# The low part of the weight last in the down units between pairs, and the sixth down weight's split moved behind the first chunk's addition

## The chip, the core and the metric

The kernel runs on one core of a Trainium2 chip. Its metric is the device time of one execution in microseconds (us). A core has five engines that matter here: PE (TensorE, matrix products into PSUM), DVE (VectorE), ACT (ScalarE), POOL (GpSimd) and SP (SyncE, which issues most loads). Each engine takes its instructions strictly in the order in which they stand in its queue, and they wait for each other by semaphores. The order in each queue is decided when the program is built.

## What is computed

One inference step of a decoder with two layers, on 512 new prompt tokens and 8 sample tokens (520 columns), width 1024:

```python
for i in range(DEPTH):                       # 2 layers: attention, then gated linear attention
    mp, ... = swa_prompt(...) / gla_mix(...)
    x = layer_norm(ALPHA * x + mix, ...)
    h = x @ w_up                             # (1024 -> 2 * 2816): gate a and value u
    c = conv_b + sum(conv_w[j] * ap[:, j:j + T] for j in range(3))
    y = (gelu(c) * u) @ w_down               # 2816 -> 1024
    x = layer_norm(ALPHA * x + y, ...)
```

All of it is in float32. What matters here is the second half of each layer, the gated feed-forward part, and the layer norm behind it.

## The kernel before

**Products.** Activations lie transposed, with the features on the partitions: 8 blocks of 128 features. Tokens are in two groups, a (256 columns) and b (264). A product of float32 precision is made of three matrix products in the fast format fp32r: a weight is split into a high part h (`wh`) and a low part l (`wl`), an activation into `hh` and `hl` (or `xh`, `xl`), and a block takes h·hh + h·hl + l·hh. A unit of work is one weight tile of 128x1024 with its two parts. Units are loaded ahead; six pairs of `wh`/`wl` buffers turn round (WSLOTS = 6), and two buffers for the raw weight.

**Two ways to a low part.** ACT copies the raw weight into `wh` (rounding it), and then either DVE subtracts (L200, L314: `wl` = raw - `wh`), or ACT writes -`wh` into `wl` (L205) and POOL issues a DMA that adds the weight from memory onto it (L206, `low_by_dma`). The weights of the down units between pairs take the second way.

**The feed-forward part.** Its 2816 features are 22 blocks j. The first four blocks are made by plain gate and value units; from j = 4 on, a gate and a value are made together by `ffn_pair` (seven half products, L308 to L310). The down product is done in five parts of 4, 4, 4, 2 and 8 blocks. The weights of the first four parts are spread over 14 units, one behind each pair from j = 4 to j = 17 (`ffn_down2`, L919 to L921). Such a unit of the first three parts makes two output chunks m and m + 1 for each group: 2 chunks x 4 blocks x 3 products = 24 matmuls into the two halves of one PSUM tile `widep`, group a and then group b, and DVE adds both halves to x at once (L924 or L926). The low product stands third for each block:

```python
for s in range(2):
    for k in range(nk):
        nc.tensor.matmul(o, h[:, ks], rh, ...)    # L919
        nc.tensor.matmul(o, h[:, ks], rl, ...)    # L920
        self.final = nc.tensor.matmul(o, l[:, ks], rh, ...)   # L921
```

**The last down products.** Behind pair 21 stand the eight units of the last part (`ffn_down`, one output chunk m each). The first four chunks of group a (the heads, L938) are begun together, and end with the products that need block 21. Then comes `ln_chunk`: DVE adds chunk m to x (L335); for m = 0 PE sums the columns of the sum (L341, tile `sc`), ACT reads that out (L343, `sb`), and DVE and POOL subtract it from x (L350). Then follow chunk 4, the chunks of group b and so on in turn. The products with the fifth and the sixth weight are L236 and L238 (high), with the low part's in one run at the end (L243).

**Releases.** Loads are not timed; a load is issued where a unit releases its buffer (`release`, `load_next`), and the split's instructions are put into the queues of ACT and DVE there. In the last pair (j = 21) releases are held back (`self.held`) and given out at its end: two behind the last addition of its products, and three (`kinds[1:]`: two units, one half buffer) behind its last instructions on ACT and DVE, by `issue_after`, which only sets the order in which a planner places instructions. So the splits of the fifth and the sixth down weight stand on DVE behind the last split of the activations.

Of the kernel before, what the change touches and what calls it, by code (L numbers as in the profile page):

```python
# [15 lines left out]
ALU = mybir.AluOpType  # L16
# [69 lines left out]
def in_turn(rows):  # L86

    return rows.rearrange("p t j -> p j t")
# [10 lines left out]
class Net:  # L99
# [226 lines left out]
    def ln_chunk(self, g, m, ps, scaled, last=False):  # L326


        nc, n, x = self.nc, g.n, g.x
        t = lambda name: self.ln.tile([P, g.n], F32, name=f"{name}_{g.name}")  # L330
        c = lambda name, b=1: self.ln.tile([P, NT - 256], F32, name=name, bufs=b)[:, :n]
        if m:
            yield 0
        if scaled:
            nc.vector.scalar_tensor_tensor(x[:, m], x[:, m], self.back[:, m:m + 1], ps, op0=ALU.add, op1=ALU.add)  # L335
        else:
            nc.vector.scalar_tensor_tensor(x[:, m], x[:, m], ALPHA, ps, op0=ALU.mult, op1=ALU.add)
        if m == 0:
            yield 1
            mp = self.mtile("sc")[:, :n]  # L340
            nc.tensor.matmul(mp, self.ones_a, x[:, 0], start=True, stop=True)  # L341
            sb = c("sb")
            nc.scalar.activation(sb, mp, AF.Copy, scale=float(KD))  # L343
            sa = sb
            if not scaled:
                sa = c("sa")
                nc.scalar.activation(sa, mp, AF.Copy, scale=KD / ALPHA)
            for i in range(KD):
                eng = nc.gpsimd if i else nc.vector
                eng.tensor_tensor(x[:, i], x[:, i], sa if i else sb, op=ALU.subtract)  # L350
            g.s2 = t("s2")
            nc.scalar.activation(g.s2, x[:, 0], AF.Square)
            return
        q = c("sq", 2)
        sq = nc.scalar.activation(q, x[:, m], AF.Square)
        if m == 6 and g.i == 0:
            with self.tc.issue_after(sq.ins):
                nc.scalar.preload_act_table_set("natural_log_exp_and_others")
        if last and m == KD - 1:

            g.q = q
            return
        if m == 1:
            g.s1 = t("s1")

        p1, p2 = (KD - 1, KD - 1) if g.i and not last else (0, S2P)
        (nc.gpsimd if m < p1 else nc.vector).tensor_tensor(g.s1, x[:, 0] if m == 1 else g.s1, x[:, m], op=ALU.add)
        (nc.gpsimd if m < p2 else nc.vector).tensor_tensor(g.s2, g.s2, q, op=ALU.add)
# [452 lines left out]
    def ffn_pair(self, u, layer, j, q):  # L821


        nc, W = self.nc, self.w[u]
        a, b = self.groups
        if j == PAIRED:
            self.plain = False
            self.row_sum1()
            self.close(self.cp_cm)
            self.cp, self.cp_cm = self.open(f"merged{layer}")  # L830
            self.m = [self.cp.tile([P, 2, 2 + NT], F32, name=f"merged{i}") for i in range(2)]
            self.c = [self.cp.tile([P, 2, NT - 256], F32, name=f"conv{i}") for i in range(2)]
            for t in self.m:
                nc.gpsimd.memset(t[:, 0, 0:2], 0.0)
            self.close_psum()
            self.open_wide()
        if j == NF - 1:
            self.held = []
        half = KD // 2
        part = lambda g, ks: (g.xh[:, ks], g.xl[:, ks])  # L840
        lo, hi = slice(0, half), slice(half, KD)
        t1, (t2, t3, t4) = part(b, lo), zip(self.th, self.tl)
        n, m = a.n, b.n
        add = lambda o, x, y: nc.vector.tensor_tensor(o, x, y, op=ALU.add)
        M, C = self.m[j % 2], self.c[j % 2]
        both = lambda x: x.unsqueeze(1).broadcast_to([P, 2, x.shape[-1]])
        g, h = M[:, 0], M[:, 1, 2:]
        p1 = self.one.tile([P, 512], F32, name="onep")
        with self.tc.issue_after(self.final) if j < PAIRED + ORDERED else ExitStack():
            self.half_product(p1, W["a11"], part(a, lo), n)  # L850
        v = self.ln.tile([P, NT - 256], F32, name="nv")[:, :n]
        nc.scalar.copy(v, p1[:, :n])
        p = self.wide()
        self.half_product(p[:, 0], W["a12"], part(a, hi), n)
        self.release()
        self.half_product(p[:, 1], W["s2"], t2, m)
        add(M[:, :, 2:2 + n], p[:, :, :n], both(v))
        nc.scalar.copy(h[:, n:m], p[:, 1, n:m])
        p = self.wide()
        products = [(p[:, 0], W["s1"], t1, m), (p[:, 1], W["a22"], t4, n)]  # L860
        for x in reversed(products) if j == PAIRED else products:
            self.half_product(*x)
        self.release()
        add(C[:, :, :n], p[:, :, :n], both(h[:, :n]))
        add(C[:, 0, n:], p[:, 0, n:m], h[:, n:m])
        p = self.wide()
        self.half_product(p[:, 0], W["s4"], part(b, hi), m)
        if j != NF - 2:
            self.release()
        self.half_product(p[:, 1], W["s3"], t3, m)  # L870
        self.release("half")
        add(M[:, :, 2 + n:], p[:, :, :m], both(C[:, 0]))
        summed = add(h[:, :n], p[:, 1, :n], C[:, 1, :n])
        w, cb = self.taps(layer, j)
        c = C.rearrange("p a b -> p (a b)")[:, :NT]
        nc.scalar.activation(c[:, :SEQ], g[:, 2:2 + SEQ], AF.Identity, scale=w(2), bias=cb)
        nc.vector.scalar_tensor_tensor(c[:, :SEQ], g[:, 1:1 + SEQ], w(1), c[:, :SEQ], op0=ALU.mult, op1=ALU.add)
        nc.vector.scalar_tensor_tensor(c[:, :SEQ], g[:, 0:SEQ], w(0), c[:, :SEQ], op0=ALU.mult, op1=ALU.add)
        nc.vector.scalar_tensor_tensor(c[:, SEQ:], g[:, 2 + SEQ:], w(2), self.base[:, j], op0=ALU.mult, op1=ALU.add)
        self.pcopy(self.nconv_p[:, j], g[:, SEQ:2 + SEQ])  # L880
        self.pcopy(self.nconv_s[:, j, :, 1], g[:, 2 + SEQ:])
        nc.scalar.activation(c, c, AF.Gelu)
        nc.vector.scalar_tensor_tensor(h, c, -1.0, h, op0=ALU.mult, op1=ALU.mult)
        self.split(a.hh[:, q], a.hl[:, q], parted(h[:, :n]))
        self.split(b.hh[:, q], b.hl[:, q], parted(h[:, n:]))
        if j == NF - 1:
            kinds, self.held = self.held, None
            done = [next(x for x in reversed(nc.cur_bb.bb.instructions) if x.engine == engine)
                    for engine in (mybir.EngineType.Activation, mybir.EngineType.DVE)]
            with self.tc.issue_after(summed.ins):  # L890
                self.release()
                self.release(kinds[0])
            with self.tc.issue_after(done[0]), self.tc.issue_after(done[1]):
                for kind in kinds[1:]:
                    self.release(kind)
            nc.scalar.dma_start(out=self.O["conv_p"][layer], in_=self.nconv_p)
            nc.scalar.dma_start(out=self.O["conv_s"][layer], in_=self.nconv_s)
            for cm in (self.cp_cm, self.pp_cm, self.fp_cm):
                self.close(cm)
            self.close_psum()  # L900
            self.open_acc()

    def ffn_down2(self, u, layer, part, i):


        nc = self.nc
        h, l = self.w[u]
        j0, j1 = FF_PARTS[part]
        nk = j1 - j0
        ms = KD // nk  # L910
        for g, m in ((g, ms * i + m) for g in self.groups for m in range(0, ms, 2)):
            ps, n = self.wide(), g.n
            for s in range(2):
                o = ps[:, s, :n].rearrange("p (j t) -> p j t", t=2)
                for k in range(nk):
                    t, q = (m % ms + s) * nk + k, self.place(j0 + k)
                    ks = slice(t * P, t * P + P)
                    rh, rl = in_turn(g.hh[:, q]), in_turn(g.hl[:, q])
                    nc.tensor.matmul(o, h[:, ks], rh, start=k == 0, stop=False)  # L919
                    nc.tensor.matmul(o, h[:, ks], rl, start=False, stop=False)  # L920
                    self.final = nc.tensor.matmul(o, l[:, ks], rh, start=False, stop=k == nk - 1).ins  # L921
            x = g.x[:, m:m + 2]
            if part == 0:
                nc.vector.scalar_tensor_tensor(x, x, ALPHA, ps[:, :, :n], op0=ALU.mult, op1=ALU.add)  # L924
            else:
                nc.vector.tensor_tensor(x, x, ps[:, :, :n], op=ALU.add)  # L926
# [566 lines left out]
```

## Time and profile before

| | us |
|---|---|
| median of 3 runs | 1099.82 |
| the three runs | 1105.21, 1098.45, 1099.82 |
| the profiled execution | 1098.55 |
| its span, first to last instruction | 1096.6 |
| PE busy | 1058.9 (97%) |
| DVE busy | 882.0 (80%) |
| ACT busy | 663.1 (60%) |
| POOL busy | 303.1 (28%) |
| mean granted TensorE clock | 0.994 |

The profiled execution took 1.95 us more than its span, for what lies around the first and the last instruction. A matmul here lasts about 0.28 us from its start to its end, but the next one starts about 0.11 us after it, so that PE's busy time says little of its pace: gaps between starts do. In a row of the time line stand start, length, engine, line, operation, tiles and shapes, the count, and in brackets the idle time before it with what ended it.

### The profile page before, as it was taken

What the parts mean: (1) busy time and instruction counts of PE and PEld (TensorE: products, weight loads), DVE (VectorE), ACT (ScalarE), POOL (GpSimd) and SP (SyncE); (2) the same over time, 40 slices, a digit from 0 to 9 for tenths busy, and PEclk for the clock granted to TensorE, in tenths of its full rate; (3) what the DMA queues carried; (4) which work ended last, traced back from release to release, by engine and by line L of the source; (5) the groups of instructions that cost most, each with busy time, mean ns of one, the idle gap of its engine ahead of it and who ended that gap; (6) DMA issues with size and microseconds to landing.
All of it is one profiled execution on the core that took longest, in us unless ns stands there. A gap on an engine that the chain in (4) does not pass through costs nothing.

```text
span 1096.6 us, 23781 instructions
## 1 busy us (share of the span) xinstructions
PE 1058.9 (97%) x9174; PEld 1031.2 (94%) x9174; DVE 882.0 (80%) x1797; ACT 663.1 (60%) x1308; POOL 303.1 (28%) x512
## 2 busy tenths in 40 slices
PE   8999999999999999999899999999999999999996
PEld 8997899999999999999799899899999999999995
DVE  7897668988778878978667678778988788888975
ACT  5677667766655665547545456458776655655643
POOL 4576562221111110274111100362221111110163
PEclk9999999999999999999999999999999999999998
DMA  7554048587777774437224364558588777774412
GB/s 233 147 173 125 21 128 207 135 215 191 180 177 178 176 174 116 124 130 204 66 74 145 115 185 136 164 170 215 134 205 197 180 174 177 175 185 116 116 66 79
DMA packets 65472, 167.44 MB, mean 153 GB/s; under 512 B 8104, under 2 KB 28624, under 8 KB 65360
## 3 DMA queue, kind: packets, MB, share of 16 engines
q1 hardware_dynamic: 50960, 119.47, 33.8%
q0 software_dynamic: 12240, 44.57, 23.1%
q10 hardware_dynamic: 2160, 1.89, 0.5%
q8 instruction: 72, 1.18, 0.4%
q14 instruction: 40, 0.33, 0.1%
HBM read 153.24 MB, written 8.47 MB: 147 GB/s over the span
## 4 chain that ended last, share of the span: by engine, by line
PE 66%; DVE 13%; DMA 10%; ACT 5%; issue 5%; SPq 1%; POOL 0%; DVEq 0%; ACTq 0%; POOLq 0%
PE widep L308 8%; PE widep L310 8%; PE widep L309 8%; PE accp L236 6%; PE accp L238 6%; PE accp L240 6%; PE widep L921 5%; PE widep L920 5%; PE widep L919 5%; DMA vb<-dv 2%; DMA wl<-in_w_up 2%; DVE wl L200 2%; PE onep L310 1%; PE onep L309 1%; PE onep L308 1%
## 5 line engine op out<-in xcount | busy, mean ns | idle before, releaser
L313 ACT ACTIVATE wh<-raw 128x1024 fp32r<-128x1024 f32 x72 | 76.2, 1061 | 98.7 <-PE widep L920 57.3
L194 ACT ACTIVATE wh<-raw 128x1024 fp32r<-128x1024 f32 (+1 forms) x92 | 96.0, 1047 | 52.3 <-PE accp L238 19.4
L309 PE MATMUL widep<-tl,wh 128*128 128x264 f32 (+1 forms) x432 | 119.1, 276 | 0.0
L310 PE MATMUL widep<-th,wl 128*128 128x264 f32 (+1 forms) x432 | 119.1, 276 | 0.0
L308 PE MATMUL widep<-th,wh 128*128 128x264 f32 (+1 forms) x432 | 119.1, 276 | 0.0
L236 PE MATMUL accp<-xh_b,wh 128*128 128x264 f32 x400 | 113.1, 283 | 2.6 <-DVE hprod L817 2.6
L240 PE MATMUL accp<-xh_b,wl 128*128 128x264 f32 x400 | 111.5, 279 | 0.0
L236 PE MATMUL accp<-xs_a,wh 128*128 128x256 f32 x400 | 106.1, 285 | 5.4 <-DVE sg L1202 2.5
L238 PE MATMUL accp<-xl_b,wh 128*128 128x264 f32 x384 | 107.5, 280 | 0.0
L206 POOL DMA_DIRECT2D wl<-in_w_down x28 | 24.3, 866 | 293.6 <-ACT wl L205 271.0
L238 PE MATMUL accp<-xs_a,wh 128*128 128x256 f32 x384 | 103.1, 284 | 0.5
L314 DVE TENSOR_TENSOR wl<-raw,wh 128x1024 fp32r<-128x1024 f32 x72 | 87.5, 1218 | 7.5 <-ACT wh L313 7.5
L205 ACT ACTIVATE wl<-wh 128x1024 fp32r<-128x1024 f32 x85 | 89.1, 1051 | 1.0
L200 DVE TENSOR_TENSOR wl<-raw,wh 128x1024 fp32r<-128x1024 f32 (+2 forms) x64 | 79.0, 1244 | 12.3 <-ACT wh L194 11.5
L236 PEld LDWEIGHTS accp<-xs_a,wh 128*128 128x128 f32 x400 | 76.7, 195 | 7.0 <-DVE sg L1202 2.9
L308 PEld LDWEIGHTS widep<-th,wh 128*128 128x128 f32 x432 | 82.1, 190 | 0.0
L309 PEld LDWEIGHTS widep<-tl,wh 128*128 128x128 f32 x432 | 82.1, 190 | 0.0
L310 PEld LDWEIGHTS widep<-th,wl 128*128 128x128 f32 x432 | 82.1, 190 | 0.0
L236 PEld LDWEIGHTS accp<-xh_b,wh 128*128 128x128 f32 x400 | 75.7, 189 | 4.3 <-DVE hprod L817 3.4
L308 PE MATMUL widep<-xh_b,wh 128*128 128x264 f32 x288 | 79.6, 276 | 0.0
L309 PE MATMUL widep<-xl_b,wh 128*128 128x264 f32 x288 | 79.5, 276 | 0.0
L310 PE MATMUL widep<-xh_b,wl 128*128 128x264 f32 x288 | 79.5, 276 | 0.0
(419 smaller groups left out, 4113.1 us busy)
## 6 DMA issues: line engine op xcount, KB each, us to landing
raw<-in_w_up SPq DMA_DIRECT2D x88, 512.0 KB, 4.0
wl<-in_w_up POOLq DMA_DIRECT2D x52, 512.0 KB, 7.1
raw<-in_w_down SPq DMA_DIRECT2D x44, 512.0 KB, 3.9
wl<-in_w_down POOLq DMA_DIRECT2D x28, 512.0 KB, 6.5
raw<-in_w_gla SPq DMA_DIRECT2D x24, 512.0 KB, 3.5
raw<-in_w_mix_o SPq DMA_DIRECT2D x16, 512.0 KB, 4.1
qs<-hl SPq DMA_DIRECT2D x64, 64.0 KB, 2.1
sgla<-in_state_gla SPq DMA_DIRECT2D x16, 256.0 KB, 2.9
```

The costliest lines, as they stand in the source:

```text
L194: nc.scalar.activation(h[:, c], r[:, c], AF.Copy)
L200: nc.vector.tensor_tensor(l[:, c], r[:, c], h[:, c].bitcast(F32), op=ALU.subtract)
L205: self.nc.scalar.activation(l, h.bitcast(F32), AF.Copy, scale=-1.0)
L236: nc.tensor.matmul(o, h[:, ks], xh, start=k == 0, stop=False)
L238: nc.tensor.matmul(o, h[:, ks], xl, start=False, stop=False)
L240: nc.tensor.matmul(o, l[:, ks], xh, start=False, stop=not tail and k == nt - 1)
L308: self.nc.tensor.matmul(o, h[:, ks], rh, start=k == 0, stop=False)
L309: self.nc.tensor.matmul(o, h[:, ks], rl, start=False, stop=False)
L310: self.final = self.nc.tensor.matmul(o, l[:, ks], rh, start=False, stop=k == KD // 2 - 1).ins
L313: self.nc.scalar.activation(hi, src, AF.Copy)
L314: self.nc.vector.tensor_tensor(lo, src, hi.bitcast(F32), op=ALU.subtract)
L919: nc.tensor.matmul(o, h[:, ks], rh, start=k == 0, stop=False)
```

## The change

Two things. In `ffn_down2`, the products of both halves with the high part come first, and those with the low part in one run at the end. And of the three releases that the last pair gave out at its end, only the first (`kinds[1]`, the fifth weight) stays there; the other two are kept and given out in `ln_chunk`, behind the addition of chunk 0 of group a.

```diff
         if scaled:
-            nc.vector.scalar_tensor_tensor(x[:, m], x[:, m], self.back[:, m:m + 1], ps, op0=ALU.add, op1=ALU.add)
+            first = nc.vector.scalar_tensor_tensor(x[:, m], x[:, m], self.back[:, m:m + 1], ps, op0=ALU.add, op1=ALU.add)
+            if m == 0 and g.i == 0:
+                with self.tc.issue_after(first.ins):
+                    for kind in self.kept:
+                        self.release(kind)
...
             with self.tc.issue_after(done[0]), self.tc.issue_after(done[1]):
-                for kind in kinds[1:]:
-                    self.release(kind)
+                self.release(kinds[1])
+            self.kept = kinds[2:]
...
-            for s in range(2):
+            for low, s in ((0, 0), (0, 1), (1, 0), (1, 1)):
...
                     rh, rl = in_turn(g.hh[:, q]), in_turn(g.hl[:, q])
+                    if low:
+                        self.final = nc.tensor.matmul(o, l[:, ks], rh, start=False, stop=k == nk - 1).ins
+                        continue
                     nc.tensor.matmul(o, h[:, ks], rh, start=k == 0, stop=False)
                     nc.tensor.matmul(o, h[:, ks], rl, start=False, stop=False)
-                    self.final = nc.tensor.matmul(o, l[:, ks], rh, start=False, stop=k == nk - 1).ins
```

Three places show what this does to the queues. PE's queue at the first `ffn_down2` unit of layer 0, group a (`widep` is the PSUM tile, `hs_a` holds the activations' two parts), before:

```order
L310 MATMUL widep_3397<-th_2730,wl_3313 128x264
L919 MATMUL widep_3530<-hs_a,wh 128x256
L920 MATMUL widep_3530<-hs_a,wh 128x256
L921 MATMUL widep_3530<-hs_a,wl 128x256
L919 MATMUL widep_3530<-hs_a,wh 128x256
L920 MATMUL widep_3530<-hs_a,wh 128x256
L921 MATMUL widep_3530<-hs_a,wl 128x256
```

The end of the same 24 products in the changed kernel, where L926, L927 and L924 are the former L919, L920 and L921 (eight such couples of L926 and L927 stand ahead of the run of eight):

```order
L926 MATMUL widep_3530<-hs_a,wh 128x256
L927 MATMUL widep_3530<-hs_a,wh 128x256
L926 MATMUL widep_3530<-hs_a,wh 128x256
L927 MATMUL widep_3530<-hs_a,wh 128x256
L924 MATMUL widep_3530<-hs_a,wl 128x256 x8
L926 MATMUL widep_3556<-hh_b,wh 128x264
```

The first use of `wl` moved from the third place to the seventeenth.

DVE's queue behind pair 21 of layer 0, at the fifth and the sixth down weight (`wl_6619`, then `wl_6625`), before:

```order
L314 TENSOR_TENSOR hl_b_93<-merged1_3383,hh_b_92 128x264
L200 TENSOR_TENSOR wl_6619<-raw_6617,wh_6618 128x1024
L200 TENSOR_TENSOR wl_6625<-raw_6623,wh_6624 128x1024
L335 SCALAR_TENSOR_TENSOR x_a_86<-x_a_86,back_85,accp_6642 128x256
L350 TENSOR_TENSOR x_a_86<-x_a_86,sb_6739 128x256
```

The same place in the changed kernel (the sixth weight's low part is now `wl_6730`, and L354 the former L350):

```order
L314 TENSOR_TENSOR hl_b_93<-merged1_3383,hh_b_92 128x264
L200 TENSOR_TENSOR wl_6619<-raw_6617,wh_6618 128x1024
L335 SCALAR_TENSOR_TENSOR x_a_86<-x_a_86,back_85,accp_6636 128x256
L200 TENSOR_TENSOR wl_6730<-raw_6728,wh_6729 128x1024
L354 TENSOR_TENSOR x_a_86<-x_a_86,sb_6739 128x256
```

The addition L335 changed places with the sixth weight's subtraction; the sixth weight's copy on ACT and its load on SP stand where they stood. Layer 1 shows the same two moves. The planner moved one more thing, in each layer: ACT's queue behind pair 16, before:

```order
L876 ACTIVATE conv_3384<-merged_3382,par 128x512
L882 ACTIVATE conv_3384<-conv_3384 128x520
L313 ACTIVATE wh<-raw 128x1024
L852 COPY nv<-onep 128x256
L313 ACTIVATE hs_a<-merged_3382 128x2x128
```

And in the changed kernel (L880, L886 and L856 are the former L876, L882 and L852):

```order
L880 ACTIVATE conv_3384<-merged_3382,par 128x512
L313 ACTIVATE wh<-raw 128x1024
L886 ACTIVATE conv_3384<-conv_3384 128x520
L856 COPY nv<-onep 128x256
L313 ACTIVATE wh<-raw 128x1024
L313 ACTIVATE hs_a<-merged_3382 128x2x128
```

There a weight's copy (L313) went ahead of the GELU, and a second one ahead of the split of block 16's product. DVE's queue follows it with the same weights' subtractions. Beside this, two transposes in the second layer's mixer stand one matmul later on PE; POOL and SP keep their order.

## The prediction

> **What bounds the kernel.** I read the page first, its busy times and the chain that ended last.
>
> ```profile
> PE 1058.9 (97%) x9174; PEld 1031.2 (94%) x9174; DVE 882.0 (80%) x1797; ACT 663.1 (60%) x1308; POOL 303.1 (28%) x512
> PE 66%; DVE 13%; DMA 10%; ACT 5%; issue 5%; SPq 1%; POOL 0%; DVEq 0%; ACTq 0%; POOLq 0%
> ```
>
> PE carries two thirds of the chain. The change takes no matmul away, so it can only shorten stretches in which PE waits. The list of PE's waits says what there is to win. Its columns are who waited for whom, the total in us, how often, and the longest.
>
> ```profile
> PE accp L236 <- DVE sg L1202: 2.5, 1, 2.5
> PE sc L341 <- DVE x_a L335: 2.5, 2, 1.4
> PE accp L236 <- ACT wh L194: 2.3, 3, 1.4
> ...
> PE widep L921 <- DMA wl<-in_w_down: 2.0, 2, 1.1
> ```
>
> Two of these rows name the places that the change touches: the low product L921 waits twice for the low part's DMA, and the column sum L341 waits twice for the addition L335. Twice each, so once per layer. That is 4.5 us in 1096.6, or 0.4%: the waits that the change touches do not hold 1%. The other two rows stand in the mixers, between the feed-forward parts; I need them below.
>
> **The down units: the first unit's wait.** The time line of PE at the first `ffn_down2` unit of each layer:
>
> ```profile
> 223.62 0.27 PE L919 MATMUL widep<-hs_a,wh 128*128 128x256 f32 x1
> 223.73 0.28 PE L920 MATMUL widep<-hs_a,wh 128*128 128x256 f32 x1
> 224.92 0.38 PE L921 MATMUL widep<-hs_a,wl 128*128 128x256 f32 x1 [0.92 <-DMA wl<-in_w_down]
> 225.14 0.28 PE L919 MATMUL widep<-hs_a,wh 128*128 128x256 f32 x1
> ...
> 227.48 0.28 PE L919 MATMUL widep<-hh_b,wh 128*128 128x264 f32 x1
> ...
> 800.08 0.27 PE L919 MATMUL widep<-hs_a,wh 128*128 128x256 f32 x1
> 800.19 0.28 PE L920 MATMUL widep<-hs_a,wh 128*128 128x256 f32 x1
> 801.57 0.38 PE L921 MATMUL widep<-hs_a,wl 128*128 128x256 f32 x1 [1.10 <-DMA wl<-in_w_down]
> 801.78 0.28 PE L919 MATMUL widep<-hs_a,wh 128*128 128x256 f32 x1
> ```
>
> From 225.14 to 227.48 there are 21 matmuls: 2.34 / 21 = 0.111 us from one start to the next. From L920 at 223.73 to the second L919 at 225.14 there are two steps, which should take 0.22 and took 1.41: the wait cost 1.19. In layer 1 it is 801.78 - 800.19 - 0.22 = **1.37**.
>
> In the changed kernel 16 high products stand ahead of the first low one: it comes up at 223.62 + 16 x 0.111 = 225.40 and at 800.08 + 1.78 = 801.86. The low part was there by 224.92 and 801.57, when L921 began. So it is early by 0.48 and 0.29, and both waits go whole. A landing later by d than this costs d minus that margin, at most what the wait cost before. The other units have nothing to give, as the group of L921 over the whole of layer 0's pairs shows: one idle stretch in 112 matmuls of group a.
>
> ```profile
> L921 PE MATMUL widep<-hs_a,wl 128*128 128x256 f32 x112 | 30.9, 276 | 0.9 <-DMA wl<-in_w_down 0.9
> ```
>
> What does the new order cost PE? It goes to and fro between the two halves of `widep` with two more switches per couple of chunks: 12 units x 2 groups + 2 units x 4 couples = 32 couples in a layer, 64 in both, 128 switches. The 21 matmuls above contain one such switch and show no step longer than 0.01 us over the pace; so 0 to 0.01 each, 0 to 1.3 us in all. Eight low products in one run exist already (L243), at (1.06 - 0.28) / 7 = 0.111 each:
>
> ```profile
> 474.88 1.06 PE L243 MATMUL accp<-hs_a,wl 128*128 128x256 f32 x8
> ```
>
> I take 0 for the order. The unit's last reader of `wh` comes 8 low products earlier, and ACT's copy of a later weight, which waits for such readers, may start some 0.9 us earlier:
>
> ```profile
> L313 ACT ACTIVATE wh<-raw 128x1024 fp32r<-128x1024 f32 x72 | 76.2, 1061 | 98.7 <-PE widep L920 57.3
> ```
>
> That ACT waits there 57.3 us in total says that it has time; PE never waits for these copies between 225.14 and 472.56, so nothing is won. DVE adds both halves at once, behind the last low product as before.
>
> **The sixth weight.** DVE and PE behind pair 21, layer 0 and then layer 1:
>
> ```profile
> 469.75 2.36 DVE L200 TENSOR_TENSOR wl<-raw,wh 128x1024 fp32r<-128x1024 f32 x2 [0.50 <-ACT wh L194]
> 472.03 0.47 DVE L335 SCALAR_TENSOR_TENSOR x_a<-x_a,back,accp 128x256 f32<-128x256 f32 x1
> 473.71 0.42 DVE L350 TENSOR_TENSOR x_a<-x_a,sb 128x256 f32<-128x256 f32 x1 [1.21 <-ACT sb L343]
> ...
> 469.87 0.28 PE L938 MATMUL accp<-hs_a,wl 128*128 128x256 f32 x1
> ...
> 470.87 0.28 PE L938 MATMUL accp<-hs_a,wl 128*128 128x256 f32 x1
> 472.56 0.70 PE L341 MATMUL sc<-x_a,ones_a 128*128 128x256 f32 x2 [1.41 <-DVE x_a L335]
> ...
> 1046.07 2.36 DVE L200 TENSOR_TENSOR wl<-raw,wh 128x1024 fp32r<-128x1024 f32 x2 [0.51 <-ACT wh L194]
> 1048.34 0.47 DVE L335 SCALAR_TENSOR_TENSOR x_a<-x_a,back,accp 128x256 f32<-128x256 f32 x1
> ...
> 1047.52 0.28 PE L938 MATMUL accp<-hs_a,wl 128*128 128x256 f32 x1
> 1048.87 0.70 PE L341 MATMUL sc<-x_a,ones_a 128*128 128x256 f32 x2 [1.08 <-DVE x_a L335]
> ```
>
> The first head ended at 469.87 + 0.28 = 470.15, so chunk 0 lay ready for 1.9 us while DVE subtracted two weights. Two subtractions took 472.03 - 469.75 = 2.28 from start to start, one takes 1.14. In the changed kernel one is left ahead: L335 starts at 470.89. PE followed 0.53 behind L335's start (472.56 - 472.03), so L341 starts at 471.42, **1.14** earlier; PE is free for it at 470.87 + 0.11 = 470.98 and still waits 0.44. In layer 1: 2.27 / 2 = **1.14** as well, L341 at 1047.73, free at 1047.63. At most the whole of these waits could go, 1.58 and 1.24.
>
> What is late next? L350 needs `sb`, 1.68 behind L335's start. The sixth subtraction now stands between: 0.4 + 1.14 = 1.54 behind that start DVE is free again, 0.14 before it is needed. Were it later, this would cost the difference, on DVE first. The sixth weight's low part is finished near 470.9 + 1.6 = 472.5; the chain has PE at the run of products that reads it here:
>
> ```profile
> 480.42 0.89 PE accp L243 x8
> ```
>
> At 479.3 in the changed kernel, then: a cover of nearly 7 us. Its copy on ACT and its load stand where they stood, so the load's start does not move against the copy.
>
> **Pair 16.** The GELU goes behind a weight's copy, about 1 us by the 1061 ns above. What hangs on it is block 16 of the last down part, which PE reads some 50 us later (pair 16 is near 400, the heads end at 470.87). Cost nothing; without that cover it would be 1.06 us per layer. The DVE moves there bring two weights forward. The two transposes in the mixer move by one matmul, 0.11 us, in a stretch where PE does other products: nothing.
>
> **The sum.** 1.19 + 1.37 + 1.14 + 1.14 = 4.84 us. Against the profiled execution's own 1098.55 this gives 1093.7; that execution lies 1.27 under the median of the three runs shown, 1099.82, against which it would be 1095.0. I predict **1094.3**, between the two. Behind each saving PE runs on at its pace, and the loads, splits and additions are released by PE's own progress, so that what it wins should move everything behind it.
>
> **Rivals.**
> *Given back in the second mixer.* Layer 0's saving, 1.19 + 1.14 = 2.33, passes through the linear attention, where PE waits 2.5 us for DVE (L1202) and 1.4 for ACT at a weight. If those waits end by loads in flight rather than by PE's progress, they grow by what was won. Then 1098.55 - 2.51 = 1096.0. For it: the waits are there and are long. Against it: the loads are released by PE and the norm ahead. 13%.
>
> *The low part's wait stays in part.* A landing later by over 0.3 to 0.5 us, from another state of the queues, gives back up to 2.56: 1096.3. For it: margins of 0.29 and 0.48 are small beside the 6.5 us that such a transfer takes from issue to landing (the last column, a median):
>
> ```profile
> wl<-in_w_down POOLq DMA_DIRECT2D x28, 512.0 KB, 6.5
> ```
> Against it: in layer 0 nothing ahead of the load has changed. 8%.
>
> *The clock.* Three stretches in the second mixer, by engine's busy time, with the granted clock in PEclk:
>
> ```profile
> 540.30:543.73 3.43, 0.90 (x7) 0.58 (x6) 2.88 (x9) 2.01 (x9) 0.13 (x1) 1.00 0.00 0
> 543.73:547.14 3.41, 3.41 (x19) 3.41 (x18) 2.46 (x5) 0.97 (x4) 3.41 (x8) 0.50 0.50 154
> 547.14:550.50 3.36, 3.36 (x32) 3.36 (x32) 2.36 (x8) 1.57 (x5) 0.58 (x2) 1.00 0.00 0
> ```
>
> After a stretch in which PE was busy for 0.90 of 3.43 us, the clock was half for 3.41 us: 19 matmuls where the next stretch has 32, some 1.7 us lost. If the shift splits the idle time otherwise, this stretch may go: 1093.7 - 1.7 = 1092.0, 12%. Or others come: the wait for ACT above, 1.4 us, and two more of that size would have to fall so. **Slower than before** it becomes from three such stretches more: 1093.7 + 3 x 1.7 = 1098.8, and 0.25 over its own time before; 4%. [...]
>
> *It doesn't do what it says.* The queues show both moves, so the waits can't stay in their old form. 1%.
>
> **How the numbers follow.** The forecast has the remaining 62%, at 1093.7 to 1095.0. The cases of a gain end at 1092.0 and 1096.3; 1.3 us of switches on top gives 1097.6; and single runs of the kernel before lay 1.37 apart in two of three, the third 5.4 higher, so that a median may sit a little above its sum. The range is 1091.0 to 1098.5. A change of 1%, 11 us, is about what a measurement of this kernel can tell from none; it would need more than twice the waits that the change touches, or on the slow side more than anything named here. Faster by over 1%: 0.02; within 1%: 0.95; slower by over 1%: 0.03.
>
> **What would show it.** In the changed profile the waits of the low product for `wl` are gone or under 0.3 us, and no other PE wait stands in the pairs' stretch; L341 waits 0.3 to 0.5 us in layer 0 and about 0.1 in layer 1; both stretches from the first down unit to L341 are shorter by 1.2 + 1.1 and 1.4 + 1.1; the mixers take the time they took, give or take a half-clock stretch. I am wrong if the first low product still waits, if L335 waits for something else than DVE's queue, or if the second mixer has become longer by what the first layer won.

## The result, and the profile after

| | before | after |
|---|---|---|
| median, us (22 runs each) | 1099.61 | **1096.16** |
| lowest and highest run, us | 1095.85, 1105.21 | 1093.50, 1099.52 |
| the profiled execution, us | 1098.55 | 1097.34 |
| its span, us | 1096.6 | 1095.5 |

The ratio is 0.9968, 95% interval 0.9960 to 0.9977: 3.5 us less, between 2.5 and 4.4. The forecast was 1094.3, from a sum of 4.84 us.

The two profiled executions differ by only 1.21 us, so I did not compare ends. I cut the span at two of PE's instructions in each layer: the first matmul of the first down unit, and the column sum of chunk 0 behind pair 21. The view that sums busy time over given stretches then gives, for the kernel before (columns: stretch, its length, busy time of PE, PEld, DVE, ACT, POOL, the granted clock, DMA share, GB/s):

```profile
223.62:472.56 248.94, 246.61 (x2199) 246.23 (x2197) 206.56 (x350) 148.95 (x219) 34.78 (x73) 1.00 0.70 173
472.56:800.08 327.52, 317.26 (x2660) 304.75 (x2661) 255.09 (x574) 193.36 (x427) 93.74 (x138) 0.99 0.51 143
800.08:1048.87 248.79, 246.61 (x2198) 246.23 (x2196) 206.76 (x350) 149.01 (x219) 33.38 (x65) 1.00 0.69 170
```

and for the changed kernel:

```profile
225.86:472.54 246.68, 246.52 (x2198) 246.22 (x2196) 205.76 (x350) 150.87 (x219) 36.15 (x73) 1.00 0.70 173
472.54:800.72 328.18, 316.71 (x2661) 303.38 (x2662) 255.94 (x575) 193.44 (x427) 94.05 (x138) 1.00 0.51 143
800.72:1047.69 246.97, 246.54 (x2198) 246.22 (x2196) 205.67 (x350) 150.94 (x219) 34.61 (x65) 1.00 0.69 170
```

The two stretches that the change touches became shorter by 2.26 and 1.82, together **4.08 us**. The stage ahead of them, whose queues are the same, took 2.24 longer (225.86 against 223.62), and the mixer between them 0.66 longer; behind the second column sum both kernels have 47.8. That adds up to the 1.2 us between the two executions, and says that an end-to-end difference of two executions can hide a gain of this size.

Now the places themselves. PE's time line of the changed kernel at the first down unit of layer 0, and the column sums of both layers:

```profile
225.86 0.27 PE L926 MATMUL widep<-hs_a,wh 128*128 128x256 f32 x1
225.97 0.28 PE L927 MATMUL widep<-hs_a,wh 128*128 128x256 f32 x1
...
227.53 0.28 PE L927 MATMUL widep<-hs_a,wh 128*128 128x256 f32 x1
227.65 0.39 PE L924 MATMUL widep<-hs_a,wl 128*128 128x256 f32 x2
...
472.10 0.28 PE L944 MATMUL accp<-hs_a,wl 128*128 128x256 f32 x1
472.54 0.70 PE L345 MATMUL sc<-x_a,ones_a 128*128 128x256 f32 x2 [0.16 <-DVE x_a L335]
...
1047.48 0.28 PE L944 MATMUL accp<-hs_a,wl 128*128 128x256 f32 x1
1047.69 0.70 PE L345 MATMUL sc<-x_a,ones_a 128*128 128x256 f32 x2
```

The low product comes 0.12 behind the last high one, without a wait. The column sum stands 0.44 and 0.21 behind the last head's matmul, where the pace is 0.11: 0.33 and 0.11 lost (the rows show the idle time alone, 0.16 and none). DVE behind pair 21, both layers:

```profile
470.87 1.23 DVE L200 TENSOR_TENSOR wl<-raw,wh 128x1024 fp32r<-128x1024 f32 x1 [0.49 <-ACT wh L194]
472.01 0.47 DVE L335 SCALAR_TENSOR_TENSOR x_a<-x_a,back,accp 128x256 f32<-128x256 f32 x1
472.40 1.22 DVE L200 TENSOR_TENSOR wl<-raw,wh 128x1024 fp32r<-128x1024 f32 x1
473.70 0.43 DVE L354 TENSOR_TENSOR x_a<-x_a,sb 128x256 f32<-128x256 f32 x1
...
1047.17 0.47 DVE L335 SCALAR_TENSOR_TENSOR x_a<-x_a,back,accp 128x256 f32<-128x256 f32 x1
1047.56 1.22 DVE L200 TENSOR_TENSOR wl<-raw,wh 128x1024 fp32r<-128x1024 f32 x1
1048.85 0.42 DVE L354 TENSOR_TENSOR x_a<-x_a,sb 128x256 f32<-128x256 f32 x1
```

One subtraction stands ahead of L335, one behind it, and L354 begins 1.69 and 1.68 behind L335, as it did before (1.68): the moved subtraction delays nothing.

What the prediction did not have is one row in the list of PE's waits of the changed kernel:

```profile
PE widep L926 <- ACT merged L862: 0.4, 1, 0.4
PE sc L345 <- DVE x_a L335: 0.2, 1, 0.2
```

A high product of a down unit waits for a copy on ACT. PE at the **second** down unit, behind pair 5, in layer 0 and layer 1:

```profile
240.55 0.28 PE L310 MATMUL widep<-th,wl 128*128 128x264 f32 x1
240.74 0.38 PE L926 MATMUL widep<-hs_a,wh 128*128 128x256 f32 x1
240.95 0.28 PE L927 MATMUL widep<-hs_a,wh 128*128 128x256 f32 x1
...
815.40 0.28 PE L310 MATMUL widep<-th,wl 128*128 128x264 f32 x1
816.11 0.38 PE L926 MATMUL widep<-hs_a,wh 128*128 128x256 f32 x1 [0.43 <-ACT merged L862]
816.32 0.28 PE L927 MATMUL widep<-hs_a,wh 128*128 128x256 f32 x1
```

From L310 to L927 are two steps, 0.22 by the pace; they took 0.40 and 0.92. So 0.18 and **0.70** are lost here (0.17 and 0.69 from the starts in ns). The kernel before had no loss at these places:

```profile
239.49 0.28 PE L310 MATMUL widep<-th,wl 128*128 128x264 f32 x1
239.60 0.27 PE L919 MATMUL widep<-hs_a,wh 128*128 128x256 f32 x1
...
816.14 0.28 PE L310 MATMUL widep<-th,wl 128*128 128x264 f32 x1
816.25 0.27 PE L919 MATMUL widep<-hs_a,wh 128*128 128x256 f32 x1
```

**Where the new wait hangs.** In each pair the first tile `widep` of `ffn_pair` is read by DVE's addition (L844 before, L848 after) and by ACT's copy of eight sample columns (L858 before, L862 after); the second down unit needs that buffer again. DVE and ACT in the changed kernel's layer 1 (raw and `sum` belong to a weight of a later pair):

```profile
806.87 0.69 DVE L259 TENSOR_TENSOR sum<-raw 128x512 f32<-128x512 f32 x1 [2.49 <-DMA raw<-in_w_up]
...
813.70 1.22 DVE L314 TENSOR_TENSOR wl<-raw,wh 128x1024 fp32r<-128x1024 f32 x1
815.17 0.68 DVE L848 TENSOR_TENSOR merged<-widep,nv 128x512 f32<-128x512 f32 x1
...
815.89 0.17 ACT L862 COPY merged<-widep 128x8 f32<-128x8 f32 x1 [1.27 <-DVE merged L848]
```

DVE waits 2.49 us for a load of the next pair's raw weight, then works without a gap, at what it does for the pair's features, for x and for three weights, to the addition at 815.17; ACT's copy follows it and ends at 816.06, and PE starts 0.05 later. From the first addition to the copy's end are 9.19 us. DVE's additions of the first unit's products to x are among this work, but they did not have to wait for PE: the only idle time of DVE in it is that for the load. So whatever the first unit saves beyond the slack that this copy had is lost again 15 us later. The kernel before shows the slack, on ACT:

```profile
238.38 0.17 ACT L858 COPY merged<-widep 128x8 f32<-128x8 f32 x1 [1.20 <-DVE merged L844]
815.69 0.17 ACT L858 COPY merged<-widep 128x8 f32<-128x8 f32 x1 [1.28 <-DVE merged L844]
```

The copies ended at 238.55 and 815.86, and the second unit began at 239.60 and 816.25: 1.05 and 0.39 ahead of PE, with 0.05 needed. The change saves 1.19 and 1.37 at the first unit.

### The profile page after: what moved, and what is told of

The parts are those of the page before. It is cut to its first block, busy times and chain, and to the rows that moved or that the text cites. A ratio compares the mean times of both kernels' runs of the same rounds, so it can differ in the third digit from the quotient of the medians.

```text
span 1095.5 us, 23783 instructions
## 1 busy us (share of the span) xinstructions
PE 1059.4 (97%) x9174; PEld 1030.3 (94%) x9174; DVE 882.4 (81%) x1797; ACT 667.2 (61%) x1308; POOL 306.1 (28%) x512
## 3 DMA queue, kind: packets, MB, share of 16 engines
q8 instruction: 72, 1.18, 0.4%
## 5 line engine op out<-in xcount | busy, mean ns | idle before, releaser
L313 ACT ACTIVATE wh<-raw 128x1024 fp32r<-128x1024 f32 x72 | 75.9, 1057 | 90.2 <-PE widep L927 44.7
L310 PE MATMUL widep<-th,wl 128*128 128x264 f32 (+1 forms) x432 | 119.1, 276 | 0.0
L236 PE MATMUL accp<-xs_a,wh 128*128 128x256 f32 x400 | 105.0, 282 | 5.8 <-ACT wh L194 2.6
L238 PE MATMUL accp<-xs_a,wh 128*128 128x256 f32 x384 | 101.9, 281 | 0.5 <-DVE xs_a L314 0.4
L310 PEld LDWEIGHTS widep<-th,wl 128*128 128x128 f32 x432 | 82.1, 190 | 0.0
L310 PE MATMUL widep<-xh_b,wl 128*128 128x264 f32 x288 | 79.5, 276 | 0.0
```

What stands on the lines that cost most here:

```text
L236: nc.tensor.matmul(o, h[:, ks], xh, start=k == 0, stop=False)
L238: nc.tensor.matmul(o, h[:, ks], xl, start=False, stop=False)
L310: self.final = self.nc.tensor.matmul(o, l[:, ks], rh, start=False, stop=k == KD // 2 - 1).ins
L313: self.nc.scalar.activation(hi, src, AF.Copy)
```

## The experiments

The theory after reading this is a **shared cover:** the two units' waits overlap, so that the first unit's gain is cut to what the load and DVE behind it allow; the column sum's gain is whole; the new order costs PE nothing. The **rivals:** the new order itself costs PE time; the two parts of the change depend on each other; or one late load in one execution made the second unit's wait.

For each profile I took from the two stretches what PE lost at the three places (start-to-start steps over the pace, whose median is 0.112, with the slow step behind a wait where there is one):

| us, layer 0 / layer 1 | stretch | first unit | second unit | column sum | rest |
|---|---|---|---|---|---|
| before | 248.93 / 248.79 | 1.18 / 1.37 | 0 / 0 | 1.57 / 1.24 | 246.18 / 246.18 |
| before, again | 248.29 / 249.16 | 0.87 / 1.04 | 0 / 0 | 1.25 / 1.95 | 246.18 / 246.18 |
| after | 246.68 / 246.98 | 0 / 0 | 0.17 / 0.69 | 0.33 / 0.11 | 246.18 / 246.18 |
| after, again | 246.70 / 246.56 | 0 / 0 | 0.20 / 0.28 | 0.33 / 0.11 | 246.18 / 246.18 |
| low last alone | 248.46 / 247.97 | 0 / 0 | 1.04 / 0.55 | 1.24 / 1.24 | 246.18 / 246.18 |
| release alone | 247.43 / 247.52 | 1.16 / 1.23 | 0 / 0 | 0.09 / 0.11 | 246.18 / 246.18 |
| first unit alone | 247.77 / 248.16 | 0 / 0 | 0.34 / 0.74 | 1.24 / 1.24 | 246.18 / 246.18 |
| addition ahead | 246.62 / 246.29 | 0 / 0 | 0 / 0 | 0.44 / 0.11 | 246.18 / 246.18 |
| addition ahead, again | 246.27 / 246.27 | 0 / 0 | 0 / 0 | 0.09 / 0.09 | 246.18 / 246.18 |
| low last by half | 246.90 / 246.56 | 0.52 / 0.29 | 0 / 0 | 0.21 / 0.09 | 246.18 / 246.18 |

The last column is the same in twenty stretches, with the old order and the new: the order of the products costs **nothing** that can be seen, against the 0 to 0.01 per switch (0 to 1.3 us) of the prediction. In all eight stretches with a wait at the second unit, ACT's copy ended 9.17 to 9.18 us behind DVE's start at the load, and PE began 0.05 behind the copy: there the load's landing and DVE's work behind it set when the second unit begins.

### The low part last, without the moved releases

```diff
-            for s in range(2):
+            for low, s in ((0, 0), (0, 1), (1, 0), (1, 1)):
```

(with the rest of `ffn_down2` as in the change; the last down products as before)

> The low part last in the down units, the releases as before. Measured by a pairs' stretch: from the first matmul of the layer's first down unit to the column sum of chunk 0 (before 248.93 us in layer 0 and 248.79 in layer 1; changed kernel 246.68 and 246.98). Theory (each wait stands by itself, and what the first unit wins is partly lost to the second unit's wait for its PSUM tile, 0.17 and 0.69): 247.9 and 248.1, and 1.7 us off the time. Rival (the new order itself costs PE time elsewhere): the stretch is short by 1.19 and 1.37 less that cost, with no wait at the second unit.

Measured: 1097.85 us median of 12, ratio 0.9984, interval 0.9972 to 0.9997 (held against the kernel before beside it, 1098.94, median of 23, as are the releases alone, the first unit alone and the addition ahead below). That is 1.1 us less rather than 1.7, and layer 0's stretch, 248.46, is longer than the 247.9 expected. PE at the second unit of this kernel, layer 0 and layer 1:

```profile
241.44 0.38 PE L922 MATMUL widep<-hs_a,wh 128*128 128x256 f32 x1 [0.78 <-ACT merged L858]
...
817.52 0.38 PE L922 MATMUL widep<-hs_a,wh 128*128 128x256 f32 x1 [0.29 <-ACT merged L858]
```

The first unit's waits are gone here too, and the second unit's wait stands in both layers, 1.04 and 0.55 us with the slow step behind it. In layer 0 that is more than in the changed kernel, and leaves little of the gain. The cause is DVE's start in that layer:

```profile
232.22 0.69 DVE L259 TENSOR_TENSOR sum<-raw 128x512 f32<-128x512 f32 x1 [2.76 <-DMA raw<-in_w_up]
```

It came 6.52 us behind the first unit's first matmul (225.70); in the changed kernel's two layers it came 5.64 and 6.15 behind (806.87 - 800.72). The wait follows the load.

### The moved releases, without the new order

```diff
-                for kind in kinds[1:]:
-                    self.release(kind)
+                self.release(kinds[1])
+            self.kept = kinds[2:]
```

(and the release behind L335, as in the change; `ffn_down2` as before)

> The sixth weight's split behind the first addition, the down units in their old order. Theory: the stretch shortens by what the column sum's wait loses in the changed kernel, 1.25 and 1.14: 247.7 and 247.65, with the low product's waits of 1.1 and 1.3 as before and no wait at the second unit; 2.4 us off the time. Rival (the two parts share a cause, so that one hides the other): less than 2 us, or the whole 3.5.

Measured: 1096.31 us median of 12, ratio 0.9976, interval 0.9965 to 0.9987. PE in layer 0, at the first unit and at the column sum:

```profile
222.56 0.28 PE L924 MATMUL widep<-hs_a,wh 128*128 128x256 f32 x1
223.73 0.38 PE L925 MATMUL widep<-hs_a,wl 128*128 128x256 f32 x1 [0.90 <-DMA wl<-in_w_down]
...
469.67 0.28 PE L942 MATMUL accp<-hs_a,wl 128*128 128x256 f32 x1
469.88 0.70 PE L345 MATMUL sc<-x_a,ones_a 128*128 128x256 f32 x2
```

The first wait is back, the second unit lost nothing (in the table above), and the column sum lost 0.09 and 0.11: the two parts act apart from each other, and without the other this one takes 1.48 and 1.13 off what the sum lost before (1.57 and 1.24). That is 2.6 us by the times, with 2.4 expected.

### The low part last in the first unit alone

```diff
+            late = part == 0 and i == 0
+            for low, s in ((0, 0), (0, 1), (1, 0), (1, 1)) if late else ((0, 0), (0, 1)):
```

(with the products below it put to this order; the releases as before)

> The low part last in the first down unit of each layer alone, all 13 others and the releases as before. Theory (the new order costs nothing in the 13 others): the same stretches as with all 14, 247.9 and 248.1, and the same wait at the second unit. Rival (the order has a price per unit, and it makes the missing 0.17 and 0.69): 247.74 and 247.42.

Measured, one run: 1097.82 us. Thirteen of fourteen units have the old order, and the second unit still waits, 0.34 and 0.74. Layer 0's stretch, 247.77, happens to lie at the rival's 247.74, but the rest of 246.18 leaves no price per unit. So the wait comes from the first unit's being faster, and the other thirteen units neither gain nor lose by their order.

### The low products half by half

```diff
-            for low, s in ((0, 0), (0, 1), (1, 0), (1, 1)):
+            for low, s in ((0, 0), (1, 0), (0, 1), (1, 1)):
```

(in all 14 units)

> The changed kernel, with the low products of each half behind that half's own high products (8 high, 4 low, 8 high, 4 low) rather than behind all sixteen. The first low product then comes up 8 x 0.111 = 0.89 us behind the first matmul of the unit instead of 1.78; in the profile of before it could begin at 1.30 (layer 0) and 1.49 (layer 1). Theory, that the first and the second down unit's waits share one cover: the first unit waits some 0.4 and 0.6 us for its low part again, and the second unit's wait for its PSUM tile shrinks by as much, since the copy that frees that tile hangs on a load and on DVE and not on the first unit. So the sum of the two units' lost time stays what the later of the two asks for: lost at both together 0.4 to 0.6 in layer 0 and 0.6 to 0.8 in layer 1 (for a load that lands as in the changed kernel's profile), stretches from the first down unit to the column sum of 246.9 to 247.1 us, layer 1 246.9 to 247.1. Rival, that each wait counts by itself: the second unit's 0.17 and 0.69 stay beside 0.4 and 0.6, together 0.6 and 1.3, stretches 247.1 and 247.6. Rival, that the order itself costs PE: fewer switches than in the change, so the stretch less its waits under 246.18 by more than 0.1.

Measured, one run: 1092.17 us. PE at the first and at the second unit of layer 0:

```profile
223.99 0.28 PE L927 MATMUL widep<-hs_a,wh 128*128 128x256 f32 x1
224.52 0.60 PE L924 MATMUL widep<-hs_a,wl 128*128 128x256 f32 x3 [0.25 <-DMA wl<-in_w_down]
...
238.42 0.28 PE L310 MATMUL widep<-th,wl 128*128 128x264 f32 x1
238.53 0.27 PE L926 MATMUL widep<-hs_a,wh 128*128 128x256 f32 x1
```

Layer 0 is as the shared cover has it: 0.52 lost at the first unit, nothing at the second, though its load had come as late as in the changed kernel's second profile, where the second unit lost 0.20. The stretch is 246.90. In layer 1 the low part came earlier than expected and cost 0.29 rather than 0.6 to 0.8, so that the stretch, 246.56, lies below the 246.9 to 247.1 expected; it is that of the changed kernel's second profile. Its time is the lowest of the ten profiled executions, but not by these stretches: its mixer took 325.86 us, the shortest of ten.

### The addition ahead of a subtraction

To take the new wait away, the release that pair 5 gives out behind the first half product of its tile `widep` is held until the addition into `merged` stands in DVE's queue. Two additions and one subtraction for weights then stand behind that addition rather than ahead of it.

```diff
         self.half_product(p[:, 0], W["a12"], part(a, hi), n)
-        self.release()
+        if j != PAIRED + 1:
+            self.release()
         self.half_product(p[:, 1], W["s2"], t2, m)
-        add(M[:, :, 2:2 + n], p[:, :, :n], both(v))
+        added = add(M[:, :, 2:2 + n], p[:, :, :n], both(v))
         nc.scalar.copy(h[:, n:m], p[:, 1, n:m])
+        if j == PAIRED + 1:
+            with self.tc.issue_after(added.ins):
+                self.release()
```

> The changed kernel, with the release in the pair ahead of the second down unit (j = 5) given out behind that pair's first addition on DVE, so that this addition stands ahead of two additions and a subtraction for the next pair's weights. Theory (the second unit waits for widep because DVE's queue, behind the landing of the next pair's raw weight, comes late to that addition): no wait at the second unit, stretches of 246.5 and 246.3, and 0.9 us off the changed kernel's time. Rival (the wait at the second unit came from one late load in that execution): stretches as in the changed kernel, 246.7 and 247.0, or as short without it in both.

Measured: 1093.89 us median of 6, ratio 0.9958, interval 0.9944 to 0.9973. DVE, ACT and PE at the second unit of layer 1:

```profile
804.46 0.69 DVE L259 TENSOR_TENSOR sum<-raw 128x512 f32<-128x512 f32 x1 [1.98 <-DMA raw<-in_w_up]
...
811.43 0.68 DVE L848 TENSOR_TENSOR merged<-widep,nv 128x512 f32<-128x512 f32 x1
...
812.15 0.17 ACT L863 COPY merged<-widep 128x8 f32<-128x8 f32 x1 [1.10 <-DVE merged L848]
...
813.49 0.28 PE L310 MATMUL widep<-th,wl 128*128 128x264 f32 x1
813.60 0.27 PE L930 MATMUL widep<-hs_a,wh 128*128 128x256 f32 x1
```

From DVE's start to the copy's end are now 812.32 - 804.46 = 7.86 us instead of 9.19, the tile is free 1.28 ahead of PE, and the wait is gone in both layers. That release alone was moved in the program; with it the planner moved some copies on ACT and one load on SP by a few places, and no product on PE. The load that DVE waits for did not come earlier: DVE starts 5.71 and 5.65 us behind the first unit, and 6.06 and 5.95 in this kernel's second profile, against 5.64 and 6.15 in the changed kernel. So the chain of DVE's work behind the load is shown to be what gave part of the gain back.

### The changed kernel and the last one side by side, and second profiles

> The changed kernel itself, a second profile and times beside the next kernel. It tells what of the stages that the change doesn't touch varies from one execution to the next. Theory, that nothing is given back there: the time from the column sum of layer 0 to the first pair of layer 1 (318.1 us before, 318.75 in the first profile of the changed kernel) falls anywhere in 316.5 to 319.3, and the stretches from the first down unit to the column sum are again 246.18 plus their waits, 246.4 to 247.4; the second unit's wait for its PSUM tile is there again in layer 1, 0.3 to 1.0. Rival, that the mixer gives back what layer 0 won: 318.6 to 318.9 again, above every profile of the kernel before. Time 1096.2, ratio 0.9965 to 0.9975.

> The changed kernel with one release (that of pair 5's first half product) behind the addition that the second down unit's PSUM tile waits for, as in e4_add_ahead, to be compared with the changed kernel on one chip. Theory: no wait at the second down unit, stretches 246.3 to 246.7, so 0.2 to 1.0 us less per layer than the changed kernel beside it: 1094 to 1095, ratio to before 0.995 to 0.9965, 1 to 2 us under the changed kernel. Rival, that the 2.3 us by which it lay under the changed kernel's time came from stages that it does not touch: no difference from the changed kernel beside it, within 0.7 us.

> The kernel before, a second profile. Theory: waits of the low product of 0.9 to 1.4 us and of the column sum of 1.2 to 1.6 in each layer, no wait at the second down unit, stretches from the first down unit to the column sum of 248.5 to 249.2 us; the stretch less its waits 246.18 as in every kernel so far; the time from layer 0's column sum to layer 1's first pair elsewhere in 316.5 to 319.3 than the 318.1 of its first profile. Rival, that the mixer's time belongs to the kernel: 318.1 within 0.2.

Measured, with the kernel before at 1099.25 (23 runs):

| | median of 12, us | ratio to before | interval |
|---|---|---|---|
| the change, again | 1097.16 | 0.9980 | 0.9966 to 0.9994 |
| addition ahead, again | 1095.26 | 0.9966 | 0.9953 to 0.9979 |

The changed kernel's gain is smaller here than expected (0.9965 to 0.9975), and its wait at the second unit of layer 1, 0.28, lies just under the 0.3 to 1.0 expected; the other kernel lies just over its 1094 to 1095. The kernel with the addition ahead is 1.9 us under the changed kernel beside it; the two intervals overlap, so that this alone would not decide it. Its stretches do: no wait at the second unit in four of four, and 492.9 and 492.5 us for both stretches together, against 493.7 and 493.3 in the changed kernel (and 497.7 and 497.5 before). By the stretches it is worth 0.7 us, the change itself 4.1.

The second profile of before, one run of 1099.64 us, misses its forecast at two places: layer 0's low product lost 0.87, so that the stretch, 248.29, is under 248.5, and layer 1's column sum lost 1.95, over the 1.6. The second shows in ACT's queue in layer 1:

```profile
1047.22 1.06 ACT L194 ACTIVATE wh<-raw 128x1024 fp32r<-128x1024 f32 x1 [0.79 <-PE accp L938]
```

The sixth weight's copy came late, so that its subtraction and L335 behind it came late too, and the column sum lost 1.95 rather than 1.24. The row names the heads, but in the first profile of before the same copy began at 1045.92, ahead of the end of every head (the first at 1046.80), so it does not need them. What it needed was its load: the last part of it landed at 1047.13, 6.2 us behind its issue, against 4.2 in the first profile. With the subtraction behind L335 such a delay no longer reaches the column sum. The kernel "half by half", which has the moved releases, met the same late load in layer 1 (6.2 us, landed at 1041.51), on ACT and DVE:

```profile
1041.59 1.06 ACT L194 ACTIVATE wh<-raw 128x1024 fp32r<-128x1024 f32 x1 [0.77 <-PE accp L944]
...
1042.00 0.47 DVE L335 SCALAR_TENSOR_TENSOR x_a<-x_a,back,accp 128x256 f32<-128x256 f32 x1
```

L335 did not wait for it, and the column sum lost 0.09. L354 began 1.83 behind L335 rather than 1.68, and what follows the column sum took 47.76 us, where all profiles have 47.75 to 47.77.

**The mixer.** The stretch from layer 0's column sum to layer 1's first unit, the same in all kernels but for two transposes that stand one matmul earlier or later, took 327.52 and 326.93 before, 328.18 and 326.60 after: no order by kernel, and a mean that differs by 0.2. To the first pair of layer 1 it took 318.11 and 317.51 before and 318.75 and 317.18 after, so neither of the two rivals on the mixer in the expectations holds. Part of its scatter is the clock. The same stretch of the changed kernel that had half clock before:

```profile
543.73:547.14 3.41, 3.20 (x29) 3.01 (x28) 2.79 (x6) 0.96 (x4) 3.41 (x9) 1.00 0.39 144
```

29 matmuls instead of 19, at full clock, although PE had been as idle in the 3.43 us ahead of it (busy for 0.89, and 0.90 before). Counted over the mixers of all profiles: no stretch of half clock in both of the changed kernel, one of "addition ahead" and "half by half" (mean 326.7 us); one in both of before, "low last alone" and "first unit alone" (327.7); two in "release alone" and the other of "addition ahead" (329.5). The latter's second one:

```profile
609.60:613.01 3.41, 3.41 (x16) 3.23 (x15) 2.12 (x6) 3.06 (x8) 0.00 (x0) 0.51 0.48 148
```

So the same kernel had none in one execution and two in another. What decides which execution has one was not shown. The lengths overlap: the changed kernel's first mixer has none and is longer, at 328.18, than three of the four with one. PE's busy time in the mixer does not overlap: 315.7 to 316.7 us with none, 316.8 to 317.3 with one, 319.4 to 319.6 with two; the idle time, 9.0 to 11.5, makes the rest of the scatter.

## Why the prediction was right, and where a step failed

- **The low part's wait goes whole.** Right: 0 in both layers of both profiles, and nothing at L924. The margins of 0.48 and 0.29 held.
- **The order costs nothing.** Right: the rest is 246.18 with either order.
- **The column sum.** Right: 0.44 and 0.10 forecast, 0.33 and 0.11 measured, so 1.24 and 1.13 us won against 1.14 each. L354 was not late.
- **Pair 16 and the moved transposes at nothing.** Nothing to the contrary: the stretch with pair 16 has the same rest.
- **"No other PE wait in the pairs' stretch", and "behind each saving PE runs on at its pace".** This step failed. The second unit waits for its PSUM tile, 0.17 and 0.69, behind a load that SP issues ahead of the saving and 9.2 us of work that follow its landing. The first unit's terms, 1.19 and 1.37, were so cut to 1.02 and 0.68. The sum is then 1.02 + 1.24 + 0.68 + 1.13 = 4.07, which is the 4.08 of the stretches. The rows for it stood in the trace of before: the copies' slack of 1.00 and 0.34 beyond the needed 0.05 bounds what the first unit can give. Taken so, with the column sums at 1.14, the forecast would have been 1.00 + 0.34 + 2.28 = 3.6, less 0.1 for each slow step behind a wait. In layer 1 DVE then started 6.15 behind the first unit rather than 6.60, which is why 0.68 was won there rather than 0.34.
- **Given back in the second mixer.** Not seen: 0.2 us between means of two, in a stage that runs from 325.9 to 330.4. Given back whole, it would leave a gain of 1.8 us, outside the first interval of 2.5 to 4.4. But executions of one kernel lie up to 4.5 us apart there, so that a part of 1 us or so can't be excluded.
- **The low part's wait stays in part.** Not so in any profile with the full order.
- **The clock.** The half-clock stretch at 543.7 did go in both profiles, as this rival had it; yet the mixer was not 1.7 us shorter. In the first of them PE's busy time there fell by 0.55 (317.26 to 316.71) and its idle time grew by 1.21. The 1.7 was too much: the means of the busy time with one such stretch and with none lie 0.8 apart. The other kernels show that it comes and goes, so I count it as scatter.
- **The time.** The measured 1096.16 lies nearer to the 1096.0 and 1096.3 of two rivals than to the forecast of 1094.3. That is chance as far as the traces tell: neither rival's mechanism shows in them. Against the 1099.61 of before, 4.08 instead of 4.84 makes 1095.5, and the 0.6 that are left lie within the interval of the gain.

What stays open: the timed gain was 3.5 and then 2.1 us (0.7 to 3.7), and the stretches say 4.1, inside the first interval and just above the second. The unchanged stages vary by 2 us and more from one execution to the next, so I don't read a further loss from it, nor can I exclude one. And why the load behind the second unit lands between 5.4 and 6.5 us behind the first unit's start, though SP issues it at the same point (0.3 to 0.4 ahead of that start), was not tried.

## What to carry to other kernels

A wait that is removed is worth what the next wait leaves of it. Go from the removed wait along the waiting engine's queue, and note at each instruction that needs another engine how long its releaser had been done; where that releaser does not start from the waiting engine's own progress, the smallest such slack caps the gain. And compare executions stage by stage between landmarks: here the two changed stages were steady to 0.01 us once their own waits were taken off, while the untouched ones moved by more than the whole gain.

## What the runs showed of the hardware

- Twenty stretches of 2196 steps from matmul to matmul took 246.18 us each without their waits, at full granted clock (1.00): PE's pace has no scatter there that these records show.
- A wait at the first or the second unit cost one slow step more: the matmul behind the one that waited came 0.21 us after it instead of 0.11 (816.11 to 816.32), even where the row shows no idle time (240.74 to 240.95).
- Switching between the two halves of a PSUM tile three times rather than once per couple of chunks cost nothing (the rest of 246.18 with either order).
- Half-clock stretches came and went between executions of one kernel (none in the mixer of one execution of "addition ahead", two in that of the other), and the mixers' means with none, one and two (326.7, 327.7, 329.5 us) rose by 1.1 and 1.8, while single mixers overlapped.
